# Neighbourhood attention in blocks of 64 queries by 192 keys instead of 128 by 256

## The chip, the cores and the metric

The kernel runs on one core of one Trainium2 chip. The metric is the device time of one execution in microseconds (us). A profile of one execution of the kernel lies beside it, with a record of every instruction of every engine: PE (TensorE, with PEld for its weight loads), DVE (VectorE), ACT (ScalarE), POOL (GpSimd) and SP (SyncE, which issues most of the DMAs).

## The reference

Two requests of 512 tokens (called s = 0 and s = 1 in the code) go through two layers. Layer 0 is an RWKV-7 recurrence in both directions, layer 1 is attention over a grid of 8 rows and 64 columns with 16 heads of 64 channels. Only the attention is touched. Each token attends to a window of 8 rows and 16 columns around it; as the grid has only 8 rows, the window is always all rows, and 16 columns:

```python
win_start = np.clip(q_cols - WIN_COLS // 2, 0, GRID_W - WIN_COLS)
valid = (kc >= win_start[..., None]) & (kc < win_start[..., None] + WIN_COLS)
...
s = jnp.einsum('bnqhd,bsnkhd->bhnqsk', qr, kr, preferred_element_type=f32)
s = jnp.where(mask, s + bias.astype(f32), NEG_INF)
p = jax.nn.softmax(s.reshape(s.shape[:4] + (-1,)), axis=-1).reshape(s.shape)
return jnp.einsum('bhnqsk,bsnkhd->bnqhd', p.astype(v.dtype), vr)
...
return (o.reshape(bsz, t, D_INNER) * jax.nn.silu(z)) @ w_o + b_o
```

A kernel may compute more keys than the window holds, as long as the bias table holds -1e30 for those outside.

## The kernel before

**Layout.** In layer 1 the tokens stand in column order: token 8c + r is grid column c, row r. A tile has 128 partitions and 512 tokens. Head pair p (two heads) has q, k and v as 128 channels by 512 tokens, head 0 in partitions 0 to 63 and head 1 in 64 to 127.

**The attention of one head pair** is the generator `heads(s, p)`. It loads a bias table of three types (left edge, middle, right edge) and q, k and v, and makes `vtok`, v with tokens on the partitions, by seven transposes of 128 tokens that start 64 apart (L1439). Then it works on blocks n = 0 to 3 of 128 queries (16 columns) with 256 keys (32 columns), two blocks at a time. For a block and a head:

- scores `sc` = q k (L1452): contraction over 64 channels, so the two heads use the two row halves of the PE array (form 64\*128), 256 columns wide;
- add bias and take the maximum (L1463, DVE), exponential (L1466, ACT), normalise (L1467 and L1468, DVE), into `sb`;
- two transposes of 128 keys into the PSUM tile `pt` (L1470), four per block, and a copy of the whole bank to `pts` (L1473, ACT);
- output into the PSUM tile `po`: for each head two products over 128 keys (L1485), the heads in the two column halves of the array (form 128\*64). They are chained so that the second block of the two comes first.

When all four blocks are done, one multiplication by the gate z (L1494) empties `po`, and `halves` splits the result into two parts `os` for the output projection (a rounded copy on ACT, L379, and the difference on DVE, L380).

Every fp32 product stands in the trace as two PE instructions (two passes); a transpose as one. All other products, the projections, are fp32r over the full array (form 128\*128, 512 columns; L430, L431 and L432 are the three terms of one such product, called G below).

**PSUM** has 8 banks in this stage: pg 2 (projections), pt 2, po 1, sc 2, pm 1.

**Order.** The recurrence (up to about 1155 us of the profile) has an order of its own, which a planner wrote with estimated times. From there on (`rest`) a scheduler orders each engine's instructions when the program is built, from estimated times, dependencies and priorities; score and output products have a raised priority (`HPA`), so they are placed as soon as their inputs are estimated ready. What is interleaved with what is set by `run`: the attention of request 0 goes beside the last projections of request 0 and the output projection of layer 0 for request 1, then comes a part without attention, and the attention of request 1 goes beside its own projections. Engines work through their order strictly, so an instruction that waits holds all behind it.

Of the kernel before, what the change touches and what calls it, by code (L numbers as in the profile page):

```python
# [13 lines left out]
AF = mybir.ActivationFunctionType  # L14
ALU = mybir.AluOpType
# [4 lines left out]
P = 128  # L20
T = 512
# [210 lines left out]
class Trunk:  # L232
# [13 lines left out]
    NAB, NX, NR, NY, NSB, NBI = 2, 2, 2, 2, 4, 2  # L246
    NAK, NZ = 1, 1
    NRR, NTM = 2, 2
    ELIM = (12, 20)
# [1175 lines left out]
    def heads(self, s, p):  # L1425

        nc = self.nc
        vt, act, gps = nc.vector, nc.scalar, nc.gpsimd
        a = lambda tag, shape=(P, T), n=1, dt=F32: self.t(tag, shape, n, dt, self.ap)
        bias = a("bias", (P, 2, 3, 256), self.NBI)  # L1430
        for h in range(2):
            self.load(bias[:, h].rearrange("p a b -> p (a b)"), self.a["rpb"][2 * p + h])
        q, k, v = (self.load(a(kind, n=2), self.sp[kind, s, p]) for kind in ("q1", "k1", "v1"))
        yield
        vtok = a("vtok", (P, 7, P), self.NK)
        for j0, j1 in ((0, 4), (4, 7)):
            ps = self.p("pm", (P, 4, P))
            for j in range(j0, j1):
                nc.tensor.transpose(ps[:, j - j0], v[:, 64 * j:64 * j + P], self.ident)  # L1439
            act.copy(vtok[:, j0:j1], ps[:, 0:j1 - j0])  # L1440
            yield
        op = self.p("po", (P, 4, P))
        cols = (0, 8, 24, 32)
        for ns in ((0, 1), (2, 3)):

            scs = self.p("sc", (P, 2, 2, 256))
            with self.tc.high_priority(self.HPA):
                last = None
                for n in ns:
                    for h in range(2):  # L1450
                        hs = slice(64 * h, 64 * h + 64)
                        one = nc.tensor.matmul(  # L1452
                            scs[:, h, n % 2], q[hs, n * P:(n + 1) * P], k[hs, 8 * cols[n]:8 * cols[n] + 256], start=True, stop=True)
                        if last is not None:
                            self.behind(one, last)
                        last = one
            pts = []
            for n in ns:
                pt = self.p("pt", (P, 2, 2, P))
                for h in range(2):  # L1460
                    sb = a("sb", (P, 256), self.NSB)
                    mx = a("mx", (P, 4), 6)
                    vt.tensor_tensor_reduce(  # L1463
                        sb, scs[:, h, n % 2], bias[:, h, (0, 1, 1, 2)[n]], 1.0, -3.0e38, op0=ALU.add, op1=ALU.max, accum_out=mx[:, 0:1])
                    vt.tensor_scalar(mx[:, 1:2], mx[:, 0:1], -1.0, None, op0=ALU.mult)  # L1465
                    act.activation(sb, sb, AF.Exp, bias=mx[:, 1:2], accum_out=mx[:, 2:3])  # L1466
                    vt.reciprocal(mx[:, 3:4], mx[:, 2:3])  # L1467
                    vt.tensor_scalar(sb, sb, mx[:, 3:4], None, op0=ALU.mult)  # L1468
                    for e in range(2):
                        nc.tensor.transpose(pt[:, h, e], sb[:, e * P:(e + 1) * P], self.ident)  # L1470
                    yield
                pts.append(a("pts", (P, 2, 2, P), self.NPT))
                act.copy(pts[-1], pt)  # L1473
                if n % 2 == 0:
                    yield
            if ns[1] == 3:
                while ("z1", s, p) not in self.sp:
                    yield
                z = self.load(a("z1"), self.sp["z1", s, p])
            with self.tc.high_priority(self.HPA):  # L1480
                last = None
                for n in ns[::-1]:
                    for e in range(2):
                        for h in range(2):
                            one = nc.tensor.matmul(  # L1485
                                op[64 * h:64 * h + 64, n], vtok[:, cols[n] // 8 + 2 * e, 64 * h:64 * h + 64], pts[n % 2][:, h, e],
                                start=(e == 0), stop=(e == 1))
                            if last is not None:
                                self.behind(one, last)
                            last = one  # L1490
            yield
        with self.tc.high_priority(self.HP[s] if p == NP - 1 else 0):
            o = self.tmp()
            vt.tensor_tensor(o, op.rearrange("p n t -> p (n t)"), z, op=ALU.mult)  # L1494
# [269 lines left out]
    def rest(self, prep, mid):  # L1764
        prep.close()
        mid.close()
        self.banks(self.stack, pg=self.PG, pt=self.PT, po=1, sc=1, pm=5 - self.PG - self.PT)
# [11 lines left out]
        a = attention()  # L1779
# [6 lines left out]
        o = self.out1(0)  # L1786
# [3 lines left out]
        n = KT * NP  # L1790
# [6 lines left out]
        x = self.x1  # L1797
# [134 lines left out]
```

## Time and profile before

| | |
|---|---|
| three runs | 1651.23, 1653.18, 1654.37 us; median 1653.18 |
| span of the profiled execution | 1657.8 us; no other time of that execution is given |
| PE busy | 1558.3 us, 94% of the span |
| stage of the attention and its projections | from about 1155 us to the end |

The span of the profile is 4.6 us (0.28%) longer than the median of the runs. In the rows, "128\*64" is the part of the PE array that an instruction uses (rows by columns), "128x512 f32" the moving operand (partitions by elements), "xN" how often. A PE row of a timeline that merges several instructions gives the start of the first and the time to the end of the last. The records overlap, since products are pipelined: the cost of one is the distance from its start to the start of the next, not its duration.

### The profile page before, as it was taken

What the parts mean: (1) busy time and instruction counts of PE and PEld (TensorE: products, weight loads), DVE (VectorE), ACT (ScalarE), POOL (GpSimd) and SP (SyncE); (2) the same over time, 40 slices, a digit from 0 to 9 for tenths busy, and PEclk for the clock granted to TensorE, in tenths of its full rate; (3) what the DMA queues carried; (4) which work ended last, traced back from release to release, by engine and by line L of the source; (5) the groups of instructions that cost most, each with busy time, mean ns of one, the idle gap of its engine ahead of it and who ended that gap; (6) DMA issues with size and microseconds to landing.
All of it is one profiled execution on the core that took longest, in us unless ns stands there. A gap on an engine that the chain in (4) does not pass through costs nothing.

```text
span 1657.8 us, 46551 instructions
## 1 busy us (share of the span) xinstructions
PE 1558.3 (94%) x18824; PEld 1195.6 (72%) x18824; DVE 1218.7 (74%) x2711; ACT 1013.3 (61%) x2025; POOL 177.9 (11%) x338
## 2 busy tenths in 40 slices
PE   7989888898999998988988999999999999999998
PEld 5867667676767776766766767777777778777776
DVE  8886668688789687886879887855677585665564
ACT  6567656766765677655665765354567665455562
POOL 0000213411101123000000111000000002100000
PEclk9999999999999899988988999999999999999999
DMA  5455578676687687664668665554765346745453
GB/s 212 157 174 175 183 259 283 212 233 224 211 257 253 193 265 255 220 219 162 222 218 266 205 227 188 185 178 129 286 216 179 109 140 206 246 159 182 163 163 103
DMA packets 176184, 336.29 MB, mean 203 GB/s; under 512 B 20928, under 2 KB 53824, under 8 KB 175968
## 3 DMA queue, kind: packets, MB, share of 16 engines
q1 hardware_dynamic: 152480, 253.07, 47.9%
q0 software_dynamic: 23488, 80.23, 13.7%
q8 instruction: 148, 2.42, 0.6%
q14 instruction: 68, 0.56, 0.1%
HBM read 227.71 MB, written 105.51 MB: 201 GB/s over the span
## 4 chain that ended last, share of the span: by engine, by line
PE 72%; DVE 9%; ACT 8%; DMA 6%; issue 4%; POOL 0%; SPq 0%; DVEq 0%; ACTq 0%; POOLq 0%
PE pm L826 8%; PE pg L430 6%; PE pg L431 6%; PE pg L432 6%; PE pm L827 6%; PE pm L828 6%; PE pf L1114 3%; DMA dab<-ab 2%; PE us L1233 2%; PE us L1213 2%; PE sc L1452 2%; PE zy L1186 2%; PE po L1485 2%; PE zy L1237 2%; PE pt L1470 2%
## 5 line engine op out<-in xcount | busy, mean ns | idle before, releaser
L826 PE MATMUL pm<-act,whi 128*128 128x512 f32 x640 | 284.7, 445 | 6.0 <-ACT whi L745 2.2
L827 PE MATMUL pm<-act,whi 128*128 128x512 f32 x640 | 258.1, 403 | 15.9 <-DVE act L773 13.2
L828 PE MATMUL pm<-act,wlo 128*128 128x512 f32 x640 | 257.2, 402 | 7.6 <-DVE wlo L747 7.6
L430 PE MATMUL pg<-act,whi 128*128 128x512 f32 x384 | 158.5, 413 | 0.2 <-DVE tmp L1408 0.2
L826 PEld LDWEIGHTS pm<-act,whi 128*128 128x128 f32 x640 | 122.8, 192 | 47.6 <-issue 10.5
L379 ACT CAST whi<-raw 128x512 fp32r<-128x512 f32 x148 | 91.5, 618 | 102.9 <-PE pg L431 65.7
L827 PEld LDWEIGHTS pm<-act,whi 128*128 128x128 f32 x640 | 123.4, 193 | 42.1 <-DVE act L773 18.3
L432 PE MATMUL pg<-act,wlo 128*128 128x512 f32 x384 | 152.5, 397 | 0.0
L431 PE MATMUL pg<-act,whi 128*128 128x512 f32 x384 | 152.4, 397 | 0.0
L828 PEld LDWEIGHTS pm<-act,wlo 128*128 128x128 f32 x640 | 123.5, 193 | 37.4 <-DVE wlo L747 10.1
L380 DVE TENSOR_TENSOR wlo<-raw,whi 128x512 fp32r<-128x512 f32 x148 | 101.2, 685 | 57.1 <-ACT whi L379 56.3
L747 DVE TENSOR_TENSOR wlo<-raw,whi 128x512 fp32r<-128x512 f32 x160 | 109.1, 685 | 42.9 <-ACT whi L745 41.7
L745 ACT CAST whi<-raw 128x512 fp32r<-128x512 f32 x160 | 98.2, 619 | 54.1 <-PE pm L827 35.8
L430 PEld LDWEIGHTS pg<-act,whi 128*128 128x128 f32 x384 | 72.3, 188 | 15.4 <-issue 3.3
L432 PEld LDWEIGHTS pg<-act,wlo 128*128 128x128 f32 x384 | 72.2, 188 | 14.9 <-issue 0.3
L431 PEld LDWEIGHTS pg<-act,whi 128*128 128x128 f32 x384 | 72.4, 189 | 14.0 <-issue 2.5
L1018 DVE TENSOR_TENSOR etmp<-N 128x30 f32<-128x30 f32 (+14 forms) x240 | 78.4, 326 | 4.1
L1020 DVE TENSOR_TENSOR N<-etmp,N 128x30 f32<-128x30 f32 (+14 forms) x240 | 78.4, 327 | 3.8
L1225 ACT COPY X<-us 64x256 f32<-64x256 f32 x128 | 47.0, 367 | 39.3 <-PE zy L1092 34.1
L1463 DVE CUSTOM_DVE_ANT_0 sb<-sc,bias 128x256 f32<-128x256 f32 x128 | 49.2, 418 | 28.2 <-PE pt L1470 20.6
L1466 ACT ACTIVATE sb<-sb,mx 128x256 f32<-128x256 f32 x128 | 64.2, 503 | 7.0 <-DVE mx L1465 6.7
L1114 PE MATMUL pf<-cab 64*64 64x128 f32 (+1 forms) x2048 | 67.2, 268 | 1.1 <-issue 1.1
(408 smaller groups left out, 3661.4 us busy)
## 6 DMA issues: line engine op xcount, KB each, us to landing
dab<-ab POOLq DMA_DIRECT2D x32, 1024.0 KB, 7.3
cab<-dab SPq DMA_DIRECT2D x64, 512.0 KB, 5.0
raw<-in_w_in_dram SPq DMA_DIRECT2D x128, 256.0 KB, 3.3
bias<-in_rpb_dram SPq DMA_DIRECT2D x32, 384.0 KB, 4.7
raw<-in_w_z_dram SPq DMA_DIRECT2D x32, 256.0 KB, 4.7
raw<-in_w_k_dram SPq DMA_DIRECT2D x32, 256.0 KB, 3.4
raw<-in_w_r_dram SPq DMA_DIRECT2D x32, 256.0 KB, 3.2
k<-dk SPq DMA_DIRECT2D x32, 256.0 KB, 4.2
```

Source lines behind the costliest of these rows:

```text
L379: self.nc.scalar.copy(hi, src)
L380: (eng or self.nc.vector).tensor_tensor(lo, src, hi.bitcast(F32), op=ALU.subtract)
L430: nc.tensor.matmul(ps, hi, x[k][0], start=(k == 0), stop=False)
L431: nc.tensor.matmul(ps, hi, x[k][1], start=False, stop=False)
L432: self.mm = nc.tensor.matmul(ps, lo, x[k][0], start=False, stop=(k == KT - 1))
L745: nc.scalar.copy(hi, raw[h])
L747: nc.vector.tensor_tensor(lo, raw.pop(h), hi.bitcast(F32), op=ALU.subtract)
L826: nc.tensor.matmul(ps, hi[:, at], xh, start=(k == 0), stop=False)
L827: nc.tensor.matmul(ps, hi[:, at], xl, start=False, stop=False)
L828: nc.tensor.matmul(ps, lo[:, at], xh, start=False, stop=(k == KT - 1))
L1018: vt.tensor_tensor(tv, N[:, q + 1:, q:q + 1].broadcast_to([P, n, q]), N[:, q:q + 1, :q].broadcast_to([P, n, q]), op=ALU.mult)
L1114: end = nc.tensor.matmul(st.f[half(a), h, 0, d, g] if st.last else st.f[half(a), h, :, d, g], ab[half(h), d, g, 2 * e[d] + 1 - a], rt if s ...
```

## The change

Blocks are still handled as tiles of 128 queries, but a tile holds two blocks of 64 queries (8 columns), a in partitions 0 to 63 and b in 64 to 127, and each has its own 192 keys (24 columns).

- **Scores**: four products per tile, one for each block and head, on the four quarters of the array (form 64\*64), 192 columns wide. The bias table is loaded in four pieces of 192 columns instead of two of 768.
- **Transposes**: the two heads' 192 keys lie beside each other in `sb` (384 columns), which takes three transposes: the first 128 keys of one head, then the last 64 of that head with the first 64 of the other, then the last 128 of the other. Three per tile instead of four, and the copy to `pts` has 384 columns instead of 512. There is an eighth transpose of v, and a second small load of v for it.
- **Output**: in the free fourth quarter of the same `pt` bank, instead of `po`. First the 128-key parts (form 128\*64): two products of 128 columns where both blocks of a tile start at the same key, else four of 64 columns. Then the 64-key parts (form 64\*64): four products of 64 columns. The chain now takes the first tile of the two first.
- **Emptying**: the output of each tile is multiplied by z as soon as it is done (or copied, if z isn't there yet), four small instructions instead of one; z is loaded earlier. `po` is gone and pt has 3 banks; a pt bank is held from the first transpose to the emptying of the output.

```diff
-    LAST = ("pg", "pg", "po", "pm")
-    PG, PT, NK, NPT = 2, 2, 2, 3
+    LAST = ("pg", "pg", "pt", "pm")
+    PG, PT, NK, NPT = 2, 3, 2, 3
...
-        bias = a("bias", (P, 2, 3, 256), self.NBI)
-        for h in range(2):
-            self.load(bias[:, h].rearrange("p a b -> p (a b)"), self.a["rpb"][2 * p + h])
-        q, k, v = (self.load(a(kind, n=2), self.sp[kind, s, p]) for kind in ("q1", "k1", "v1"))
+        bias = a("bias", (P, 2, 3, 192), self.NBI)
+        rpb = self.a["rpb"][2 * p:2 * p + 2].rearrange("h p c -> p h c")
+        for ty, ps, c in ((0, slice(0, P), 0), (1, slice(0, 64), 256), (1, slice(64, P), 320), (2, slice(0, P), 576)):
+            self.load(bias[ps, :, ty], rpb[ps, :, c:c + 192])
...
+        v = a("v1", (P, T + 64), 2)
+        self.load(v[:, 0:T], self.sp["v1", s, p])
+        self.load(v[:, T:], self.sp["v1", s, p][:, 0:64])
...
-                        one = nc.tensor.matmul(
-                            scs[:, h, n % 2], q[hs, n * P:(n + 1) * P], k[hs, 8 * cols[n]:8 * cols[n] + 256], start=True, stop=True)
+                    for ab in range(2):
+                        for h in range(2):
+                            hs, c = slice(64 * h, 64 * h + 64), 64 * first(n, ab)
+                            bound(nc.tensor.matmul(
+                                scs[64 * ab:64 * ab + 64, h, n % 2, 0:192], q[hs, 64 * (2 * n + ab):64 * (2 * n + ab) + 64], k[hs, c:c + 192],
+                                start=(n % 2 == 0), stop=True, skip_group_check=True))
...
-                    for e in range(2):
-                        nc.tensor.transpose(pt[:, h, e], sb[:, e * P:(e + 1) * P], self.ident)
+                    for e in range(x, 2 * x + 1):
+                        nc.tensor.transpose(pt[:, e], sb[:, e * P:(e + 1) * P], self.ident)
...
-                act.copy(pts[-1], pt)
+                act.copy(pts[-1], pt[:, 0:3])
+                outs.append(pt[:, 3])
...
-                for n in ns[::-1]:
-                    for e in range(2):
-                        for h in range(2):
-                            one = nc.tensor.matmul(
-                                op[64 * h:64 * h + 64, n], vtok[:, cols[n] // 8 + 2 * e, 64 * h:64 * h + 64], pts[n % 2][:, h, e],
-                                start=(e == 0), stop=(e == 1))
+                for n, pt, op in zip(ns, pts, outs):
+                    halves = [(0, 0, P)] if first(n, 0) == first(n, 1) else [(0, 0, 64), (1, 64, P)]
+                    for ab, c0, c1 in halves:
+                        for x in range(2):
+                            hs = slice(64 * ((n + x) % 2), 64 * ((n + x) % 2) + 64)
+                            bound(nc.tensor.matmul(
+                                op[hs, c0:c1], vtok[:, first(n, ab) + x, hs], pt[:, 2 * x, c0:c1], start=(ab == 0), stop=False,
+                                skip_group_check=True))
+                for ab in range(2):
+                    cs = slice(64 * ab, 64 * ab + 64)
+                    for x in range(2):
+                        for n, pt, op in zip(ns, pts, outs):
+                            hs, rows, c = slice(64 * ((n + x) % 2), 64 * ((n + x) % 2) + 64), slice(64 * x, 64 * x + 64), first(n, ab)
+                            bound(nc.tensor.matmul(
+                                op[hs, cs], vtok[rows, (c + 2, (c - 1) % 8)[x], hs], pt[rows, 1, cs], start=False, stop=True,
+                                skip_group_check=True))
+            for n, op in zip(ns, outs):
+                cs = slice(n * P, n * P + P)
+                if z is None:
+                    act.copy(o[:, cs], op)
+                else:
+                    vt.tensor_tensor(o[:, cs], op, z[:, cs], op=ALU.mult)
```

`bound` ties each product behind the one before it; `first(n, ab)` is the block's first key divided by 64, between 0 and 5.

**What the change does to the order.** The order of the recurrence is the same. In the stage behind it the PE's order changes as in two places below. In the changed kernel, L1463 is the scores, L1481 the transposes, L1500 the 128-key parts and L1508 the 64-key parts of the output, L1443 the transposes of v; L472 and L458 are small sums of a norm.

PE in the attention of request 1, at the last output products of a head pair, before (pg and act, whi are a projection; one row of an fp32 product is two instructions of the trace):

```order
L430 MATMUL pg_20407<-act_18682,whi_20403 128x512
L1485 MATMUL po_20190<-pts_20375,vtok_20169 64x128 [waits Activation_49]
L1485 MATMUL po_20190<-pts_20375,vtok_20169 64x128 x3
L1485 MATMUL po_20190<-pts_20342,vtok_20169 64x128 x4
L1452 MATMUL sc_20502<-k_3852_20470,q_3851_20468 128x256 [waits DMAHW6_49,DMAHW2_49]
L1452 MATMUL sc_20502<-k_3852_20470,q_3851_20468 128x256 x3
L431 MATMUL pg_20407<-act_18681,whi_20403 128x512
```

The eight output products of two blocks stand together, and the next pair's scores right behind them. PE in the same part of the changed kernel, where pt_20399 and pt_20448 are the first two tiles of a pair and pt_20514 the third:

```order
L431 MATMUL pg_20535<-act_18728,whi_20527 128x512
L1500 MATMUL pt_20448<-pts_20474,vtok_20367 64x64 [waits Activation_49]
L1500 MATMUL pt_20448<-pts_20474,vtok_20367 64x64 x3
L1508 MATMUL pt_20399<-pts_20443,vtok_20367 64x64
L1508 MATMUL pt_20448<-pts_20474,vtok_20367 64x64
...
L432 MATMUL pg_20535<-act_18748,wlo_20528 128x512
L1500 MATMUL pt_20514<-pts_20553,vtok_20367 64x64 [waits Activation_49]
L1500 MATMUL pt_20514<-pts_20553,vtok_20367 64x64 x3
L430 MATMUL pg_20535<-act_18785,whi_20527 128x512
```

The 128-key parts of a first tile now stand alone among the projections (those of pt_20399 came some 20 rows earlier in the same way), and those of the second go together with the 64-key parts of both. PE a little later, with the pair's last tile pt_20558:

```order
L432 MATMUL pg_20622<-act_18785,wlo_20615 128x512
L1463 MATMUL sc_20719<-k_3791_20685,q_3790_20683 64x192 [waits DMAHW6_49,DMAHW3_49]
L1463 MATMUL sc_20719<-k_3791_20685,q_3790_20683 64x192 x5
L1500 MATMUL pt_20558<-pts_20584,vtok_20367 64x128 [waits Activation_49]
L1500 MATMUL pt_20558<-pts_20584,vtok_20367 64x128
L1508 MATMUL pt_20514<-pts_20553,vtok_20367 64x64
...
L1463 MATMUL sc_20719<-k_3791_20685,q_3790_20683 64x192 x2
L430 MATMUL pg_20622<-act_18804,whi_20618 128x512
```

Here the output products stand inside the next pair's scores, so the array's form changes four times between two projections.

PE at the end of request 0's attention, before (os is the finished attention of the last pair, pg its output projection):

```order
L1485 MATMUL po_18310<-pts_18428,vtok_18292 64x128 [waits Activation_49]
L1485 MATMUL po_18310<-pts_18428,vtok_18292 64x128 x3
L1485 MATMUL po_18310<-pts_18407,vtok_18292 64x128 x4
L472 MATMUL pm_18528<-tmp_18514,ones 128x128 [waits DVE_49,Activation_49]
L472 MATMUL pm_18528<-tmp_18514,ones 128x128 [waits DVE_49] x2
L430 MATMUL pg_18459<-os_18443,whi_18455 128x512 [waits Activation_49]
```

Only the norm's sums stand between the last output products and the projection that needs them. The same place of the changed kernel:

```order
L1500 MATMUL pt_18529<-pts_18546,vtok_18418 64x64 [waits Activation_49]
L1500 MATMUL pt_18529<-pts_18546,vtok_18418 64x64 x3
L1481 MATMUL pt_18548<-cc,sb_18549 128x128 [waits DVE_49]
L1481 MATMUL pt_18548<-cc,sb_18549 128x128 x2
L1500 MATMUL pt_18548<-pts_18565,vtok_18418 64x128 [waits Activation_49]
L1500 MATMUL pt_18548<-pts_18565,vtok_18418 64x128
L1508 MATMUL pt_18529<-pts_18546,vtok_18418 64x64
L1508 MATMUL pt_18548<-pts_18565,vtok_18418 64x64
...
L430 MATMUL pg_18600<-os_18584,whi_18596 128x512 [waits Activation_49]
```

The last tile's transposes moved behind the projections that covered them, and no other work stands between them, their copy, the output and the projection.

Counted over the whole stage, the products of the attention and the changes of the array's form are:

| | before | changed |
|---|---|---|
| scores | 128 of 256 columns, 64\*128 | 256 of 192 columns, 64\*64 |
| transposes of the weights | 256 | 192 |
| transposes of v | 112 | 128 |
| output | 256 of 128 columns, 128\*64 | 64 of 128 and 128 of 64 columns, 128\*64; 256 of 64 columns, 64\*64 |
| visits to another form than 128\*128 | 44 (17 begin in 64\*128) | 59 |
| further changes of form inside a visit | 24 (19 into 64\*128, 5 into 128\*64) | 69 (46 into 64\*64, 23 into 128\*64) |

More of the change, by code (lines that the diff above doesn't have):

```diff
@@ L1434, in heads @@
+        q, k = (self.load(a(kind, n=2), self.sp[kind, s, p]) for kind in ("q1", "k1"))
+        v = a("v1", (P, T + 64), 2)
+        self.load(v[:, 0:T], self.sp["v1", s, p])
+        self.load(v[:, T:], self.sp["v1", s, p][:, 0:64])
         yield
-        vtok = a("vtok", (P, 7, P), self.NK)
-        for j0, j1 in ((0, 4), (4, 7)):
+        vtok = a("vtok", (P, 8, P), self.NK)
+        for j0 in (0, 4):
             ps = self.p("pm", (P, 4, P))
-            for j in range(j0, j1):
-                nc.tensor.transpose(ps[:, j - j0], v[:, 64 * j:64 * j + P], self.ident)
-            act.copy(vtok[:, j0:j1], ps[:, 0:j1 - j0])
+            for j in range(4):
+                nc.tensor.transpose(ps[:, j], v[:, 64 * (j0 + j):64 * (j0 + j) + P], self.ident)
+            act.copy(vtok[:, j0:j0 + 4], ps)
@@ L1766, in rest @@
         mid.close()
-        self.banks(self.stack, pg=self.PG, pt=self.PT, po=1, sc=1, pm=5 - self.PG - self.PT)
+        self.banks(self.stack, pg=self.PG, pt=self.PT, sc=1, pm=6 - self.PG - self.PT)
         self.gt = "pg"
```

46 lines of the change are left out of this document (23 added, 23 removed).

## Prediction

> **What bounds the kernel now.** I began with the page's busy times, then took the stage that the change touches by the view of windows, which splits it at the end of request 0's attention.
>
> ```profile
> PE 1558.3 (94%) x18824; PEld 1195.6 (72%) x18824; DVE 1218.7 (74%) x2711; ACT 1013.3 (61%) x2025; POOL 177.9 (11%) x338
> 1155.00:1330.00 175.00, 170.38 (x1066) 133.54 (x1065) 116.19 (x417) 113.41 (x268) 5.41 (x10) 1.00 0.57 190
> 1330.00:1650.00 320.00, 319.53 (x1732) 253.35 (x1731) 195.21 (x553) 172.55 (x374) 26.00 (x48) 1.00 0.54 174
> ```
>
> In the last two rows the columns behind the length are busy PE, PEld, DVE, ACT and POOL, the granted clock (1.00) and the DMA share. PE has work in 170 of 175 us and in all but 0.5 of 320 us; DVE is busy 66% and 61% of the two, ACT 65% and 54%. So PE sets the pace from 1155 us on, and a busy PE says nothing about how much of it is needed: what counts is the distance between starts. The view of waits for PE in this stage shows how little it stands still; its three longest rows (in us, times, longest) are
>
> ```profile
> PE po L1485 <- ACT pts L1473: 1.2, 1, 1.2
> PE pm L472 <- DVE tmp L468: 1.1, 1, 1.1
> PE pg L430 <- ACT oa L1508: 0.8, 1, 0.8
> ```
>
> The first lies at the start of request 0's attention, the others at its end. The sum below is therefore one of PE slots, plus what changes in such waits.
>
> **Prices of the PE.** All come from the view of the timeline for PE. A projection product (G) and a transpose, in the same form:
>
> ```profile
> 1457.29 0.40 PE L432 MATMUL pg<-act,wlo 128*128 128x512 f32 x1
> 1457.52 0.38 PE L1470 MATMUL pt<-cc,sb 128*128 128x128 f32 x2
> 1457.66 0.48 PE L430 MATMUL pg<-act,whi 128*128 128x512 f32 x1
> 1457.97 0.40 PE L431 MATMUL pg<-act,whi 128*128 128x512 f32 x1
> ```
>
> G takes 0.23 (1457.29 to 1457.52). From 1457.29 to 1457.97 are 0.68, less two G 0.22: a transpose costs 0.11, and mixing it with G costs nothing more. Output products alone among G, and then output with scores behind:
>
> ```profile
> 1410.23 0.40 PE L430 MATMUL pg<-act,whi 128*128 128x512 f32 x1
> 1410.56 1.09 PE L1485 MATMUL po<-pts,vtok 128*64 128x128 f32 x16
> 1411.58 0.50 PE L431 MATMUL pg<-act,whi 128*128 128x512 f32 x1
> 1411.92 0.39 PE L432 MATMUL pg<-act,wlo 128*128 128x512 f32 x1
> ...
> 1417.86 0.39 PE L432 MATMUL pg<-act,wlo 128*128 128x512 f32 x1
> 1418.18 1.09 PE L1485 MATMUL po<-pts,vtok 128*64 128x128 f32 x16
> 1419.20 1.14 PE L1452 MATMUL sc<-k,q 64*128 64x256 f32 x8
> 1420.27 0.50 PE L430 MATMUL pg<-act,whi 128*128 128x512 f32 x1
> 1420.60 0.39 PE L431 MATMUL pg<-act,whi 128*128 128x512 f32 x1
> ...
> 1454.63 0.40 PE L432 MATMUL pg<-act,wlo 128*128 128x512 f32 x1
> 1454.96 1.13 PE L1452 MATMUL sc<-k,q 64*128 64x256 f32 x8
> 1456.02 0.50 PE L430 MATMUL pg<-act,whi 128*128 128x512 f32 x1
> 1456.36 0.39 PE L431 MATMUL pg<-act,whi 128*128 128x512 f32 x1
> ```
>
> Sixteen output instructions run as eight pairs on the two column halves. 1410.23 to 1411.92 less two G is 1.23; I take 0.11 a pair, as for a transpose of the same 128 columns, so 0.88, and the visit to the other form costs 0.35. Scores are four pairs on the row halves: 1454.63 to 1456.36 less two G is 1.27; at twice the columns twice the price, 0.216 a pair (0.108 is the price of 128 columns with one digit more) or 0.86 in all, and the visit costs 0.41. Both together, 1417.86 to 1420.60 less two G, are 2.28, less 0.88 and 0.86 leaves 0.54: the second change inside a visit costs 0.19. Of that, 0.09 is the gap (1418.18 to 1419.20 is 1.02 = 0.88 + 0.05 for a slow first step + 0.09) and 0.10 the slow first step of the scores. A change into 128\*64, whose first step loses only 0.05, then costs 0.14.
>
> For 64\*64 I go back to the recurrence, which uses this form at the full clock:
>
> ```profile
> 798.46 0.27 PE L1213 MATMUL us<-Z,MT 64*64 64x64 f32 x1
> 798.47 0.27 PE L1092 MATMUL zy<-cab 64*64 64x64 f32 x1
> ...
> 798.94 0.22 PE L1092 MATMUL zy<-cab 64*64 64x64 f32 x1
> 798.98 1.05 PE L1114 MATMUL pf<-cab 64*64 64x128 f32 x32
> 799.96 0.50 PE L826 MATMUL pm<-act,whi 128*128 128x512 f32 x1
> ```
>
> Between 798.46 and 798.98 run 32 instructions of 64 columns, so eight fours on the four quarters in 0.47 beside the slow first step: 0.058 a four. The 32 of 128 columns take 0.98 less the gap of 0.09: 0.111 a four. Products of 64 columns in form 128\*64 are here (both kinds, 16 instructions in eight pairs):
>
> ```profile
> 483.51 0.69 PE L1233 MATMUL us<-X,Tm 128*64 128x64 f32 x16
> 484.02 0.64 PE L1237 MATMUL zy<-X,R 128*64 128x64 f32 x16
> ```
>
> 0.51 less 0.05 over eight pairs: 0.058 a pair.
>
> **The change part by part, on PE.** Counts are those of the two orders.
>
> - Transposes of the weights: 64 fewer at 0.11, -7.0 us. Transposes of v: 16 more, +1.8.
> - Scores: before, 128 products in two passes are 128 pairs at 0.216, 27.6. After, 256 products in two passes are 128 fours of 192 columns. No row has 192 columns; by the 128-column four it is 0.111 x 1.5 = 0.167, and 21.3 in all: -6.3. Bounds: 0.111 (nothing for the added columns, -13.4) and two pairs of 0.167 (no fours, +15.1). The rows of L1114 are fours in exactly this order of quarters, so I take 0.167.
> - Output: before, 256 pairs at 0.11, 28.2. After, 64 pairs of 128 columns (7.0), 128 pairs of 64 columns at 0.058 (7.4), and 256 products in two passes, 128 fours at 0.058 (7.4): 21.8, so -6.4.
>
> That is -17.9 us of products. Against it stand the changes of form. Before: 44 visits at 0.35 (15.4), 17 of them 0.06 dearer (1.0), 19 inner changes at 0.19 (3.6) and 5 at 0.14 (0.7): 20.7. After: 59 visits at 0.35 (20.7) and 69 inner changes at 0.14 (9.7): 30.4. So **+9.7**, more than half of what the smaller products save, because the first tile's 128-key products are placed alone and the output falls into two forms. For an inner change between 128\*64 and 64\*64 no clean row exists; its bounds are the gap alone, 0.09 (3.5 less), and the dearest seen, 0.19 (3.5 more). Net on PE: -8.2.
>
> [...]
>
> **Waits.** At the end of request 0's attention the order puts the last tile's transposes, copy and output one behind the other with nothing beside them. Before, that place is
>
> ```profile
> 1323.29 1.09 PE L1485 MATMUL po<-pts,vtok 128*64 128x128 f32 x16
> 1325.46 0.91 PE L472 MATMUL pm<-tmp,ones 128*128 128x128 f32 x6 [1.08 <-DVE tmp L468]
> 1326.13 0.71 PE L430 MATMUL pg<-os,whi 128*128 128x512 f32 x2
> ```
>
> From the end of the output (1324.3) to the projection are 1.8 us, 0.7 of them filled with the sums. After, the same 1.8 (two small multiplications instead of one large) have no sums in them, and ahead of them stand an exposed copy (0.59 for 512 columns by the row below, some 0.45 for 384, an estimate, and its start and end) and a short wait for the bank: +1.5 us. Elsewhere I add nothing. The other engines' work, by the view of groups of this stage:
>
> ```profile
> L1473 ACT COPY pts<-pt 128x512 f32<-128x512 f32 x64 | 36.8, 587 | 32.0 <-PE pt L1470 31.9
> L1463 DVE CUSTOM_DVE_ANT_0 sb<-sc,bias 128x256 f32<-128x256 f32 x128 | 49.2, 418 | 28.2 <-PE pt L1470 20.6 <-PE sc L1452 7.4
> L1494 DVE TENSOR_TENSOR tmp<-po,z 128x512 f32<-128x512 f32 x16 | 11.0, 688 | 10.2 <-PE po L1485 10.0
> L380 DVE TENSOR_TENSOR wlo<-raw,whi 128x512 fp32r<-128x512 f32 x115 | 78.8, 686 | 52.9 <-ACT whi L379 52.5 <-PE po L1485 0.3 <-DMA v<-dv 0.2
> ```
>
> DVE and ACT get shorter softmax steps and copies (a quarter fewer columns) and four short multiplications for one of 0.69; both have a third of their time free, and both stay behind PE. SP issues three more DMAs per pair (two of bias, one of v), 48 in all, but carries a quarter less bias; the DMA share of 0.57 and 0.54 hides them. The bias load waits for DVE to free its buffer as before, with weight loads queued behind it on SP; those run ahead of PE. The z loads come up to half a pair earlier, after the previous pair's last multiplication; late z would hold DVE, then a pt bank, then PE, but half a pair is 8 us or more.
>
> Sum: -8.2 + 1.5 = -6.7 us. It is made in the profiled execution (span 1657.8); that span is 4.6 us above the median of the runs, all in the same clock in this stage, so I set it against the median: 1653.2 - 6.7 = **1646.5**.
>
> **Rivals.**
>
> - *The saving is eaten on PE itself.* If two row halves that write one bank go one after the other, the 64-key parts run as pairs: 128 fours become 256 pairs, +7.4 us, 1653.9, no change. Inner changes at 0.19 instead of 0.14 (+3.5) give 1650.0, at the edge of no change. For it: 75 more changes of form, none of the commonest kind timed cleanly. Against: the rows at 798.46 and the first steps seen above. Together 0.20.
> - *The bank becomes the wait.* A pt bank is now held until DVE has multiplied its output, and the second tile of each half needs the bank of the half before. If DVE is then in a weight split (0.686, L380), PE stands for it: 32 halves x 0.69 = 22 us, 1668. It decides from 0.21 us a half (6.7/32). For it: DVE is two thirds busy and works in order. Against: in the order, seven or more projection products (1.6 us) mostly stand between an output and the transposes that want its bank, and now PE waits for DVE in only one place above 1 us. 0.13, at 1657 to 1668.
> - *More gain*: the new order puts projections between the first softmax steps of request 0, where PE now waits 1.2 us for a copy and a little more around it; without these waits, and with inner changes at 0.09, 1641. This lies inside my own case.
>
> **How the numbers follow.** My case has 0.67, with a range of its own from 1641 (bounds of the inner change and the first waits) to 1649.8. About 0.2% (3.3 us) is what a measurement can tell from no change, so faster means below 1649.9: 0.67. No change: 0.20. Slower: 0.13. The range that should hold 8 in 10 goes from 1641 to 1656, into the first rival and up to where the second begins.
>
> **What would show it.** In the profile after: 64\*64 scores of 16 instructions at about 0.65 us between first and last form change, 64-key parts of 16 in about 0.25, inner changes at 0.14; about 190 changes of form in the stage; the PE's waits of the stage still under 10 us, with a new one at the end of request 0's attention. It would be wrong if fours run as pairs, if rows "PE pt <- DVE" of several us appear among the waits, or if the split of the output products costs much more than 0.14 a change.

## The result, and the profile after

The changed kernel takes 1662.64 us (median; 1660.97 to 1664.44) against 1653.18 us before: a ratio of 1.006, with a 95% interval of 1.0041 to 1.0078. It is slower by 9.5 us where 6.7 us less were forecast, and the time lies outside the range.

The view of windows on the changed kernel, over the two stretches that the prediction used (columns: length, busy PE, PEld, DVE, ACT, POOL, granted clock, DMA share, GB/s):

```profile
1155.00:1330.00 175.00, 163.31 (x1339) 124.89 (x1337) 121.83 (x460) 113.36 (x277) 5.40 (x10) 0.96 0.59 185
1330.00:1650.00 320.00, 318.75 (x2020) 248.54 (x2021) 174.72 (x546) 161.68 (x365) 26.11 (x48) 0.99 0.52 163
```

PE was busy in 170.4 of the first 175 us before; now in 163.3, and the granted clock, 1.00 before, is 0.96. The second row is nearly as it was. So the loss lies in request 0's attention. Points that both programs pass place it better than a window can. The timeline of PE has the first scores, and the transpose `pt<-cc,h` with which request 1's own part begins (called the first transpose by token), first in the kernel before, then in the changed one:

```profile
1182.83 1.13 PE L1452 MATMUL sc<-k,q 64*128 64x256 f32 x8
1366.30 0.49 PE L1529 MATMUL pt<-cc,h 128*128 128x128 f32 x3
```

```profile
1178.67 0.88 PE L1463 MATMUL sc<-k,q 64*64 64x192 f32 x16
1371.31 0.60 PE L1556 MATMUL pt<-cc,h 128*128 128x128 f32 x4
```

From the one to the other were 183.5 us and are 192.6 (+9.2); from there to the end of the span (1657.8 and 1660.9) 291.5 and 289.6 (-1.9). The whole attention and what follows took 475.0 us and takes 482.2 (+7.3). The changed kernel comes to its first scores 4.2 us earlier, though the change does nothing ahead of them: by the clock's records TensorE ran at half clock for 78.5 us ahead of 1155 us in the one execution and for 68.3 us in the other. That is why the experiments below are compared from the first scores on, beside their times.

The view of waits for PE in the changed kernel, from 1155 us to the end, in full:

```profile
PE pt L1481 <- DVE oz L1516: 4.8, 2, 4.3
PE pg L430 <- ACT os L379: 4.1, 1, 4.1
PE pt L1500 <- ACT pts L1484: 2.1, 2, 1.5
PE pg L430 <- ACT oa L1535: 0.9, 1, 0.9
PE pg L431 <- DVE os L380: 0.9, 1, 0.9
```

12.8 us in all, against 5.0 before by the same view. The long ones lie at one place, the end of request 0's attention. The timeline of PE there:

```profile
1307.66 1.16 PE L472 MATMUL pm<-tmp,ones 128*128 128x128 f32 x8
...
1312.89 0.45 PE L1500 MATMUL pt<-pts,vtok 128*64 128x64 f32 x8
1317.69 0.90 PE L1481 MATMUL pt<-cc,sb 128*128 128x128 f32 x3 [4.35 <-DVE oz L1516]
1320.08 0.69 PE L1500 MATMUL pt<-pts,vtok 128*64 128x128 f32 x4 [1.49 <-ACT pts L1484]
1320.71 0.71 PE L1508 MATMUL pt<-pts,vtok 64*64 64x64 f32 x16
1325.55 1.22 PE L430 MATMUL pg<-os,whi 128*128 128x512 f32 x2 [4.14 <-ACT os L379]
```

The number in brackets is the idle time ahead of the row, and what ended it. PE wants a bank for the last tile's transposes (L1481), and the bank is free only when DVE has multiplied the output in it (L1516). What DVE does meanwhile, by its timeline:

```profile
1310.85 2.73 DVE L1378 SCALAR_TENSOR_TENSOR h<-h,cv,acc 128x512 f32<-128x512 f32 x4
1313.49 2.73 DVE L1378 SCALAR_TENSOR_TENSOR hh<-hh,cv,acc 128x512 f32<-128x512 f32 x4
1316.14 1.29 DVE L1379 TENSOR_TENSOR h<-h,xr 128x512 f32<-128x512 f32 x2
1317.35 0.28 DVE L1516 TENSOR_TENSOR oz<-pt,z 128x128 f32<-128x128 f32 x1
...
1324.18 0.29 DVE L1516 TENSOR_TENSOR oz<-pt,z 128x128 f32<-128x128 f32 x1
```

The output that the multiplication of 1317.35 takes up left PE at 1312.9. Ten instructions of request 1's layer norm stand ahead of it on DVE, 6.5 us, and the others are spread among more norm work. In the kernel before, the norm comes last on DVE:

```profile
1324.43 0.69 DVE L1494 TENSOR_TENSOR tmp<-po,z 128x512 f32<-128x512 f32 x1 [1.98 <-PE po L1485]
...
1325.82 0.69 DVE L380 TENSOR_TENSOR os<-tmp,os 128x512 fp32r<-128x512 f32 x1
1327.71 2.74 DVE L1378 SCALAR_TENSOR_TENSOR h<-h,cv,acc 128x512 f32<-128x512 f32 x4 [1.21 <-ACT acc L476]
```

There the norm's multiplication L1378 still waits for the norm's statistics, whose sums (L472) are on PE at 1325.46, behind the last output. In the changed kernel they are at 1307.66, ahead of the last tile's transposes, so the norm can start early, and the scheduler has put it first.

A second loss lies behind the first. In the record of this trace the granted clock is 0.50 from 1315.20 to 1335.68. The view of windows, with that stretch of 20.48 us cut into six (columns as above, the clock third from the end):

```profile
1311.78:1315.20 3.42, 1.56 (x34) 0.95 (x32) 3.42 (x6) 0.00 (x0) 0.00 (x0) 1.00 0.00 0
...
1328.85:1332.26 3.41, 2.46 (x7) 1.46 (x6) 3.41 (x6) 3.41 (x8) 0.00 (x0) 0.50 0.40 108
1332.26:1335.68 3.42, 3.42 (x10) 2.65 (x9) 2.23 (x4) 1.63 (x3) 0.00 (x0) 0.50 0.79 235
1335.68:1339.09 3.41, 3.41 (x17) 2.78 (x16) 0.69 (x1) 1.14 (x2) 0.00 (x0) 1.00 0.35 104
```

In these rows 10 instructions fill a window at a clock of 0.50 (from 1332.26), and 17 the next at 1.00. The kernel before has 1.00 throughout here (in all four windows from 1320.07 to 1333.72).

### The profile page after: what moved, and what is told of

Its sections match the earlier page's. It is cut to its first block, busy times and chain, and to the rows that moved or that the text cites. A ratio compares the mean times of both kernels' runs of the same rounds, so it can differ in the third digit from the quotient of the medians.

```text
span 1660.9 us, 47855 instructions
## 1 busy us (share of the span) xinstructions
PE 1555.2 (94%) x19416; PEld 1186.9 (71%) x19416; DVE 1211.3 (73%) x2758; ACT 1003.7 (60%) x2029; POOL 178.0 (11%) x338
## 4 chain that ended last, share of the span: by engine, by line
PE 49%; DVE 6%; issue 4%; DMA 4%; ACT 4%; POOL 0%; DVEq 0%; SPq 0%; ACTq 0%; POOLq 0%
PE pg L430 6%; PE pg L431 6%; PE pg L432 6%; PE pm L826 5%; PE pm L828 4%; PE pm L827 4%; PE pf L1114 2%; DMA dab<-ab 2%; PE sc L1463 2%; PE us L1233 2%; PE us L1213 1%; PE zy L1186 1%; PE pt L1500 1%; PE zy L1237 1%; PE pt L1481 1%
## 5 line engine op out<-in xcount | busy, mean ns | idle before, releaser
L826 PEld LDWEIGHTS pm<-act,whi 128*128 128x128 f32 x640 | 122.4, 191 | 49.0 <-issue 10.2
L747 DVE TENSOR_TENSOR wlo<-raw,whi 128x512 fp32r<-128x512 f32 x160 | 109.0, 685 | 41.9 <-ACT whi L745 41.8
L1477 ACT ACTIVATE sb<-sb,mx 128x192 f32<-128x192 f32 x128 | 57.1, 449 | 12.8 <-DVE mx L1476 12.8
L430 PE MATMUL zy<-act,whi 128*128 128x512 f32 x128 | 52.3, 411 | 9.8 <-ACT whi L379 8.8
```

Source lines behind the costliest of these rows:

```text
L430: nc.tensor.matmul(ps, hi, x[k][0], start=(k == 0), stop=False)
L747: nc.vector.tensor_tensor(lo, raw.pop(h), hi.bitcast(F32), op=ALU.subtract)
L826: nc.tensor.matmul(ps, hi[:, at], xh, start=(k == 0), stop=False)
```

## The experiments

The theory to be tested: the loss is this one place, by two steps, the stand of PE behind the norm's DVE work and the halved clock that the stand brings. Its rivals: the changes of form ate the saving everywhere (A); the clock falls by itself (B). All nine experiments in one table. "To request 1" is the time from the first scores to the first transpose by token, "to the end" from the first scores to the end of the span, both from the profiled execution, with the difference to the kernel before. They are of one execution each: from the first scores to the last output products of request 0, where experiments 4 to 7 have the same PE work as the kernel before, the five traces have 140.3 to 141.6 us. The ratio is to the kernel before, run beside it; its median was 1651.25 to 1651.67 us beside the experiments, so the ratios and not the medians are compared with it.

| kernel | median us | ratio, 95% interval | to request 1 | to the end |
|---|---|---|---|---|
| before | 1653.18 | 1 | 183.5 | 475.0 |
| changed | 1662.64 | 1.006 (1.0041 to 1.0078) | 192.6 (+9.2) | 482.2 (+7.3) |
| 1 norm held back | 1648.87 | 0.9986 (0.9971 to 1.0001) | 178.4 (-5.0) | 470.7 (-4.3) |
| 2 waits filled | 1657.45 | 1.0038 (1.0022 to 1.0054) | 188.6 (+5.1) | 478.0 (+3.1) |
| 3 norm held back, second tile first | 1640.25 | 0.9941 (0.992 to 0.9961) | 176.6 (-6.9) | 461.8 (-13.2) |
| 4 before, 12 repeats | 1664.05 | 1.0083 (1.0061 to 1.0104) | 195.3 (+11.8) | 485.1 (+10.2) |
| 5 before, 12 repeats, filled | 1661.22 | 1.0063 (1.0039 to 1.0087) | 193.5 (+10.1) | 485.2 (+10.2) |
| 6 before, 6 repeats | 1656.36 | 1.0021 (1.0001 to 1.0041) | 191.2 (+7.7) | 481.9 (+6.9) |
| 7 before, 3 repeats | 1655.96 | 1.0024 (1.0009 to 1.0039) | 187.3 (+3.9) | 477.5 (+2.6) |
| 8 changed, second tile first | 1655.32 | 1.0024 (1.0008 to 1.0039) | 190.3 (+6.8) | 476.5 (+1.5) |
| 9 norm held back, scores whole | 1648.30 | 0.9975 (0.996 to 0.9991) | 181.7 (-1.8) | 470.5 (-4.5) |

### 1: the norm held back

```
 def halves(...):
-    (eng or self.nc.vector).tensor_tensor(lo, src, hi.bitcast(F32), op=ALU.subtract)
+    self.sub = (eng or self.nc.vector).tensor_tensor(lo, src, hi.bitcast(F32), op=ALU.subtract)
 # heads, at its end
     o = self.halves(o, lo, hi)
+    self.ev = self.sub
 # norm0
-    nc.vector.scalar_tensor_tensor(h, h, self.vec("post0", k), rstd, ...)
+    one = nc.vector.scalar_tensor_tensor(h, h, self.vec("post0", k), rstd, ...)
+    self.behind(one, self.ev)
```

> The changed kernel with one order fixed: the eight VectorE multiplications of the next layer norm (L1378) have to stand behind the subtraction that ends the last head pair of request 0, so the pair's four small output multiplications are no longer queued behind 5.5 us of norm work. Theory (the loss is at this one place): in the changed kernel TensorE waits 10.9 us there against 4.6 before, and the granted clock is 0.5 from 1315.3 to 1335.7, in which some 9 us of products run at half speed, 4.5 us more. Both go: 1662.6 - 6.3 - 4.5 = 1652, between 1648 and 1654, clock 1.0 through the whole attention. Rival A (the form changes on TensorE ate the saving): the time stays at 1659 to 1664 although the waits are gone. Rival B (the clock falls by itself, whatever TensorE waits): the waits go, a halved stretch of some 20 us stays, 1656.

1648.87 us, 13.8 us below the median of the changed kernel, which was run at another time (by the two ratios some 12 us); against the kernel before, the interval just includes no change. The same place in the timeline of PE (lines are one higher than in the changed kernel), and of DVE:

```profile
1309.34 0.45 PE L1501 MATMUL pt<-pts,vtok 128*64 128x64 f32 x8
...
1311.35 0.46 PE L1509 MATMUL pt<-pts,vtok 64*64 64x64 f32 x16
1313.12 1.22 PE L430 MATMUL pg<-os,whi 128*128 128x512 f32 x2 [1.31 <-ACT os L379]
```

```profile
1311.93 0.49 DVE L1517 TENSOR_TENSOR oz<-pt,z 128x128 f32<-128x128 f32 x2 [1.98 <-PE pt L1509]
...
1313.71 2.73 DVE L1378 SCALAR_TENSOR_TENSOR h<-h,cv,acc 128x512 f32<-128x512 f32 x4
```

From the last tile but one's products (L1501, 1309.34) to the projection are 3.8 us; in the changed kernel they were 12.7 (1312.89 to 1325.55). The norm starts 6.4 us later than it did against that row of PE, and no wait for it appears among PE's waits up to request 1. Of the halved stretch one window of 3.4 us is left. So the changed program is 5.0 us shorter than the kernel before up to request 1 as soon as this place is mended, and rival A is out as the explanation. Rival B, with its 20 us of half clock left over, is out too. To the end the gain is -4.3 and not -6.7: one wait of 2.0 us is in request 1's last pair (L1501 for the copy L1485), where the changed kernel waits 0.6 and the kernel before not at all.

### 2: the waits filled

```
+    if s == 0 and p == NP - 1 and n == 2:     # behind the last tile but one's 128-key products
+        for i in range(9):
+            bound(nc.tensor.matmul(scs[:, i % 2, 0], self.ident, self.scan[0][:, 0:256], start=False, ...))
     ...                                        # and once more behind the last 64-key product
```

> The changed kernel with nothing moved, but 2 x 9 dummy products of 128x256 (some 0.44 us each, into score columns that nobody reads any more; they are extra work, no part of the result) put on TensorE into the two long waits at the end of request 0's attention. The waits of the real products stay as they are. Theory: the halved clock is TensorE's idleness; filled, the clock stays at 1.0 and the time falls by the clock's share alone, 4.5 us: 1658, between 1656 and 1660. Rival B (the clock falls for another reason): the halved stretch stays, and the time is 1662 to 1666. Rival A says nothing of this run but no gain: 1662.

1657.45 us, as the theory said, though the intervals of the two ratios overlap (1.0022 to 1.0054, and 1.0041 to 1.0078), and the rows, which are of the fastest of its ten executions, have to tell them apart. The real products wait as before, but TensorE is at work; the timeline of PE, and the window over the place:

```profile
1306.39 4.15 PE L1505 MATMUL sc<-cc 128*128 128x256 f32 x18
...
1313.46 4.15 PE L1516 MATMUL sc<-cc 128*128 128x256 f32 x18
1317.26 0.81 PE L430 MATMUL pg<-os,whi 128*128 128x512 f32 x2
```

```profile
1302.00:1325.00 23.00, 18.33 (x123) 13.71 (x124) 22.12 (x42) 14.83 (x28) 0.00 (x0) 1.00 0.34 102
```

The clock is 1.00, and up to request 1 the stretch is 4.1 us shorter (188.6 against 192.6) by work that is good for nothing. That is the clock's share of the loss: the two projection products here are 0.81 us, in the changed kernel 1.22. Rival B falls: keeping TensorE busy was enough.

### 3: the norm held back, and the second tile's output first

```
 # as 1, and in heads
-    for n, pt, op in zip(ns, pts, outs):            # the 128-key products
+    for n, pt, op in list(zip(ns, pts, outs))[::-1]:
```

> The first experiment's order, and the output products of a pair's second tile issued ahead of the first's, so that two tiles' products of one form meet: the program has 136 changes of form instead of 187 in the attention, 51 visits away from the full array instead of 59, 34 changes inside a visit instead of 69. By the prediction's prices that is 8 x 0.35 + 35 x 0.15 = 8 us less than the first experiment: 1644, between 1640 and 1647. Rival A (form changes cost much more than the prediction's prices and ate the saving): 15 us or more below the first experiment. Rival C (a tile's bank becomes the wait, since the second tile's probabilities come later than the first's): no faster than the first experiment.

1640.25 us, 0.9941 of the kernel before (0.992 to 0.9961): faster than both. From the first scores to the end it is 9.0 us below the first experiment, where the prices of the changes of form gave 8; some 2.3 us of it may be chains of scores, of which this order breaks one and the others eight (experiment 9), which that 8 leaves out. In the timeline of PE the first tile's 128-key products no longer stand alone, and an output visits the other forms once (12 instructions of 128\*64, then 16 of 64\*64):

```profile
1394.65 0.67 PE L1501 MATMUL pt<-pts,vtok 128*64 128x64 f32 x12
1395.26 0.46 PE L1509 MATMUL pt<-pts,vtok 64*64 64x64 f32 x16
```

### 4 to 7: the same two steps in the kernel before

If the theory holds, the loss can be made in the kernel that does not have it. The last output multiplication of request 0 is carried out 13, 7 or 4 times, with the norm held behind it as in 1; in experiment 5, TensorE gets 20 dummy products meanwhile. Where the sixth and the seventh expectation count in windows, these are stretches of 3.41 us as in the changed kernel's rows; that a window less than half busy brings the halved clock is an estimate of mine from the row with 1.56 us of work in 3.42 (46%) there.

```
-    vt.tensor_tensor(o, op.rearrange("p n t -> p (n t)"), z, op=ALU.mult)
+    for _ in range(13 if s == 0 and p == NP - 1 else 1):     # 4: 13, 6: 7, 7: 4
+        vt.tensor_tensor(o, op.rearrange("p n t -> p (n t)"), z, op=ALU.mult)
```

> The kernel before, in which the last output multiplication of request 0 (128x512, 0.69 us) is carried out 13 times instead of once, and the norm's VectorE work is held behind it: TensorE has to wait 12 x 0.69 = 8.3 us longer there, and nothing else is changed (its result is the same). Theory: 8.3 us of waiting and a halved clock behind it that costs 2 to 5 us more: 1653.2 + 8.3 + 4 = 1665, between 1663 and 1668, with a stretch of clock 0.5 where the kernel before has none. Rival B (the clock has nothing to do with the wait): 1661.5 and clock 1.0 there.

> The fourth experiment (the last output multiplication of the kernel before carried out 13 times) with 20 dummy products of 128x256, 0.44 us each, put on TensorE between the last attention product and the out projection that waits, so that TensorE works through the 8.3 us instead of standing; they write columns that nobody reads any more. Theory: the real products wait as long as in the fourth experiment, but the clock stays at 1.0: before + 8.3, some 1660, and 3.5 us less than the fourth. Rival B (the clock falls for another reason): as the fourth, before + 12.

> As the fourth experiment with 6 repeats more instead of 12: 4.1 us of waiting on top of the 2.2 us that the kernel before has there. [...] A stand of 6 us holds such a window wherever the grid lies, and the price is that of one or two windows at half speed, nearly as in the fourth experiment: before + 4.1 + 2 to 4, some 1658. If the halved stretch grew with the wait (half of the fourth's 3.5) it would be before + 5.9; if the clock has nothing to do with it, before + 4.1.

> As the fourth with 3 repeats more: 2.1 us of waiting on top of 2.2 us. With the clock rule of the sixth experiment the stand of some 4 us may or may not leave a window less than half busy, by where the grid lies in each execution: before + 2.1 in some, before + 2.1 + 2 to 4 in others. With no clock effect: before + 2.1.

Windows of 3.41 us around the place, laid by where the record's clock changes, for 12 repeats, then for 3 repeats:

```profile
1325.80:1329.22 3.42, 0.00 (x0) 0.00 (x0) 3.25 (x6) 0.00 (x0) 0.00 (x0) 0.50 0.00 0
...
1332.63:1336.04 3.41, 3.39 (x9) 2.27 (x8) 3.41 (x6) 2.49 (x5) 0.00 (x0) 0.50 0.00 0
1336.04:1339.46 3.42, 3.42 (x16) 2.80 (x16) 3.42 (x6) 1.96 (x4) 0.00 (x0) 1.00 0.00 0
```

```profile
1312.02:1315.44 3.42, 2.34 (x24) 1.71 (x23) 1.48 (x6) 0.00 (x0) 0.00 (x0) 1.00 0.24 77
1315.44:1318.85 3.41, 1.34 (x9) 0.79 (x7) 2.66 (x5) 1.20 (x2) 0.00 (x0) 1.00 0.00 0
1318.85:1322.26 3.41, 3.39 (x8) 2.22 (x8) 3.41 (x7) 2.52 (x5) 0.00 (x0) 0.50 0.00 0
```

The halved clock is there each time, for 3 windows with 12 repeats, 2 with 6, 1 with 3, and with the filler (experiment 5) for none. So at this place it is TensorE's standing that brings it, in either kernel. The two rows that bracket the wait in experiments 4 and 5, output and projection:

```profile
1319.98 1.09 PE L1486 MATMUL po<-pts,vtok 128*64 128x128 f32 x16
...
1331.87 1.22 PE L430 MATMUL pg<-os,whi 128*128 128x512 f32 x2 [8.59 <-ACT os L379]
```

```profile
1315.87 1.09 PE L1486 MATMUL po<-pts,vtok 128*64 128x128 f32 x16
1316.89 8.90 PE L1494 MATMUL sc<-cc 128*128 128x256 f32 x40
...
1327.88 0.74 PE L430 MATMUL pg<-os,whi 128*128 128x512 f32 x2 [1.19 <-ACT os L379]
```

11.9 and 12.0 us: the same wait. Behind it the filled one is faster by 1.7 us up to request 1 (193.5 against 195.3), where I had expected 3.5. The size was wrong, because most of the halved stretch lies over time in which TensorE has no work: only the window from 1332.63, and 0.8 us of work ahead of it, run at half speed. To the end the two are equal (485.1 and 485.2), since the unfilled variants are 0.8 to 1.6 us shorter than the kernel before in the stage of request 1 and the filled one is not; I did not follow that up. The two ratios overlap too, so the times by themselves do not tell 4 from 5; the clock in the rows does.

With 6 and 3 repeats the stage is longer by 7.7 and 3.9 us, for 4.1 and 2.1 us of repeats: 3.6 and 1.8 us more than the repeats, and with 12 repeats 3.5. So from 6 to 12 repeats the surplus does not grow with the wait, as the sixth expectation said. It is not the clock alone, though: the filled variant, at full clock, has 1.8 us of it too. PE's rows divide it. From the first scores to the last output products, where nothing is changed, are 140.5 us in the kernel before and 141.5, 141.6, 140.9 and 140.3 in experiments 4 to 7, so up to 1.1 us of the surplus has nothing to do with the repeats. From there to the projection the four take 0.8, 0.9, 0.6 and 0.5 us more than the kernel before and the repeats at 0.69. From the projection to request 1, where the clock acts, are 40.2 us before and 39.9 with the filler, but 41.8, 42.7 and 41.7 with 12, 6 and 3 repeats. So the clock's price is 1.5 to 2.5 us, and three repeats bring nearly as much of it as twelve.

### 8: the second tile first, with the norm left where it was

The third experiment's second edit alone.

> The changed kernel with the output products of a pair's second tile issued ahead of the first's (as in the third experiment), and the norm's VectorE work left where it was, ahead of the last multiplications. Theory: the form changes give the 8.5 us that they gave between the first and the third experiment, and the waits and the halved clock at the end of request 0 stay: changed kernel - 8.5, so some 0 to 1 us above the kernel before. If the two loss sources were one (fewer changes of form also end the waits), it would be near the third experiment, 1640.

1655.32 us: 5.7 us less than the changed kernel by the stretch to the end, where I had expected 8.5. The view of waits up to 1330 us has

```profile
PE pt L1481 <- DVE oz L1516: 5.1, 1, 5.1
PE pg L430 <- ACT os L379: 5.0, 2, 4.7
```

against 4.8 and 4.1 in the changed kernel, and by the timeline the half clock is there again: three transposes take 0.90 us at 1314.59 and 0.58 at 1305.60, a projection product 0.63 at 1329.19 and 0.39 at 1307.62. TensorE comes to the place earlier and stands there 1.2 us longer, because DVE's work sets when the place ends. So here a gain ahead of a place that another engine holds is in part given back. The rest of the missing 2.8 us isn't in these two waits: over the whole stage the view has 16.2 us of waits against 12.8, the longest new one 1.2 us for a load of v (L1443).

### 9: the norm held back, and no chain of scores broken

One term of the prediction's sum had no answer yet. It counted the scores as 128 fours. In the changed kernel's order, output products are put into the middle of 8 of the 32 chains of scores:

```
 # as 1, and in heads
-    with self.tc.high_priority(self.HPA):           # around the scores
+    with self.tc.high_priority(self.HPA + 1000):
```

> The first experiment, with the scores' products given a higher priority than the output's, so that no output is put into the middle of a chain of scores. In the changed kernel's order 8 of the 32 chains of eight scores are broken by an output (6 and 2, or 7 and 1), so that fours become lone products and pairs: 16 steps of 0.164 us more, 2.6 us, which the prediction's 128 fours left out. Now none is broken, and the changes of form stay the same (186 for 187; 62 visits for 59, 62 inner changes for 69). Theory: from the first scores to the end 470.7 - 2.6 = 468 us on the trace, and some 1646. If broken chains cost nothing: 470.7 as in the first experiment.

The timeline of PE at such a chain in the changed kernel, and then of the same work in this experiment:

```profile
1421.27 0.39 PE L430 MATMUL pg<-act,whi 128*128 128x512 f32 x1
1421.59 0.88 PE L1463 MATMUL sc<-k,q 64*64 64x192 f32 x14
...
1423.06 0.49 PE L1463 MATMUL sc<-k,q 64*64 64x192 f32 x2
...
1423.81 0.39 PE L432 MATMUL pg<-act,wlo 128*128 128x512 f32 x1
```

```profile
1436.63 0.39 PE L432 MATMUL pg<-act,wlo 128*128 128x512 f32 x1
1436.95 0.88 PE L1464 MATMUL sc<-k,q 64*64 64x192 f32 x16
...
1438.86 0.39 PE L431 MATMUL pg<-act,whi 128*128 128x512 f32 x1
```

Less two G, the broken one takes 2.08 us (1421.27 to 1423.81) and the whole one 1.77 (1436.63 to 1438.86): 0.31 a chain, the price expected of two steps of 0.164. But the stretch to the end is 470.5 us, not 468: in request 1 and behind it 3.4 us are gained against the first experiment (five chains, and its 2.0 us wait), and in request 0 as much is lost, where the new order has two halved windows instead of one and 1.5 us more of waits. So the price of a broken chain is shown where it stands; that mending them makes the whole faster is not (1648.30 and 1648.87 us).

## Why the prediction was wrong

**The prices held in the rows that show them.** Fours of 192 columns, an estimate of 0.167 without a row of their own, follow each other at 0.164. The two row halves do write one bank together, as us<-Z,MT does in the kernel before (798.46): 16 instructions of the 64-key parts are 0.46 long in the first experiment's rows, slow first step and last one's tail included. And the block of 128-key products, 64-key parts and whole scores, which by the prediction's prices (one visit, two inner changes) is 1.75 us, is 1.77. So the first rival (the saving eaten on PE itself) did not come true, and with the norm held back the stage up to request 1 is 5.0 us shorter than before.

**The step that failed is "Waits": "+1.5 us" and "Elsewhere I add nothing".** The view of waits has 12.8 us against 5.0, so +7.8. I had the place right, the end of request 0's attention, and put it down to PE, its copies and "two small multiplications instead of one large". I read the order on PE there and not the one on DVE, which shows the norm's eight multiplications (L1378) ahead of the last four of the output (L1516). The mechanism was among my rivals (a bank held until DVE has multiplied its output), but I had priced it as a weight split of 0.69 us in each of 32 halves and given it 0.13; it is 6.5 us of another stage's work in one half. That 1662.6 lies inside the 1657 to 1668 of this rival is therefore luck: there it was many short waits all through the attention, here it is one place and the clock. The sentence on what would make the prediction wrong, rows of "PE pt <- DVE" of several us, is what the profile shows, and the waits are above the 10 us that it named.

**The clock was not a term at all.** The granted clock of 1.00 in the rows of before was taken as given. In the changed kernel it is 0.50 for 20.48 us behind and in PE's stand; the second experiment puts this share at 4.1 us.

**The count of steps was too good**: 8 of 32 chains of scores are broken in the changed order, 16 steps of 0.164, +2.6 us (0.31 of 0.33 a chain measured at one of them). The 128 pairs of the kernel before left out the same: 3 of its 32 chains are broken behind the first or the third of their four products, 2 more steps of 0.216 each, 1.3 us. (In one of them PE takes 2.91 us from 1588.78 to 1592.15, less two G; the prediction's whole one takes 2.28, and by its prices 0.20 of the 0.63 are changes of form that the count has.) So this term is worth +1.3 us.

Together: -6.7 + 6.3 (waits beyond the 1.5) + 4.1 + 1.3 = +5.0 us, against +7.3 in the traces from the first scores on. The 2.3 us left are not explained. The times say +9.5 (6.8 to 12.9 by the interval).

## What to carry to other kernels

Where a change splits an operation into small parts and lets a bank or a buffer wait for them, read the order of the engine that frees the bank, not only of the one that fills it: at the seam of two stages the next stage's bulk work may stand ahead of the small part, and here one explicit order (the norm behind the last output) was worth more than the split itself. And price a stand of TensorE with what follows it: here the long ones cost their length and then the clock, and with short pieces of work between stands (4.35, 1.49 and 4.14 us) the clock was 0.50 for six windows of 3.41 us, where one whole stand of 8.6 us had three (experiment 4).

## What the hardware showed that was not expected

The halved clock did not need a window without work. In the changed kernel the last window ahead of it has 1.56 us of work (46%), and with 3 repeats 1.34 us (39%): there a wait of 2.1 us beside one of 1.1 us stood ahead of a halved window (experiment 7). Behind the 2.34 us (68%) of the window before that one, the clock stayed at 1.00. It was back at 1.00 behind windows of 3.39 us (3 and 12 repeats) and 3.42 us of work (the changed kernel, from 1332.26), but stayed at 0.50 behind the 2.46 us (72%) from 1328.85, and behind the full window from 854.40 of the same trace. Nor does the share of one window decide the fall: in the kernel before, the clock is 0.50 behind the window from 538.41 with 2.52 us of work (74%), and 1.00 behind the one from 316.55 with 1.56 us (46%, as much as in the changed kernel at 1311.78). So a limit such as the half of my estimate is not shown by these traces.
